# The last norm of a hybrid decoder block: rows on VectorE alone, fetched by GpSimd's queue, the last bias one expert sooner

## The chip, the cores and the metric

The kernel runs on one core of a Trainium2 chip. The time is the device time of one execution in microseconds (us); the median of three executions stands for the kernel. A profile of one execution, taken on the chip, gives the trace that is read here. Engines are named as the profile names them: PE (TensorE), PEld (its weight loads), DVE (VectorE), ACT (ScalarE), POOL (GpSimd), and SP (SyncE, which only issues DMAs here). SPq and POOLq are the DMA queues of these engines.

## The reference, cut to what matters

The block takes 512 tokens of 1024 features through a token mixer and a norm, then through a mixture of 32 experts of which each token uses 4, adds a gate by an input embedding (`ple`), and ends with a layer norm over all 1024 features:

```python
def expert_block(args):
    toks, e = args
    xb = x_pad[toks]
    hgu = xb @ w_gate_up[e] + b_gate_up[e]
    gate = jnp.minimum(hgu[:, :D_FF], SWIGLU_LIMIT)
    up = jnp.clip(hgu[:, D_FF:], -SWIGLU_LIMIT, SWIGLU_LIMIT)
    act = (up + 1.0) * gate * jax.nn.sigmoid(SWIGLU_ALPHA * gate)
    return act @ w_down[e] + b_down[e]
...
    ple = jax.nn.sigmoid(h @ w_ple_gate[i]) * (p[i].astype(h.dtype) @ w_ple_proj[i])
    h = layer_norm(DN_ALPHA * h + y + ple, ln_moe_g[i], ln_moe_b[i])
```

`y` is the sum over a token's four experts, weighted by the router. All is float32.

## The kernel before

The first third of the time is the token mixer. From about 700 us on, a loop runs over 32 places `e`; at each place one expert is done, in an order that a sort of the experts by their number of tokens gives (`RANKS`). A place is long (a first block of 64 tokens and a second of 32) or short (the first block alone); `SHORT_AT` lists the 13 short places, which take the experts with the fewest tokens. A block of 64 tokens fills PE by halves: the two halves of a weight's columns go to the two halves of the output's 128 partitions.

At each place SP loads 12 units of 1024 KB: 8 with the rows of `w_gate_up` (128 input features each) and 4 of `w_down`. The units go round 18 buffers, so SP runs ahead of PE. PE multiplies units 1 to 4 in order. In a short place the last four units are then multiplied twice, first for the left 256 columns and then for the right (`LATE`), so that ACT and DVE can work on the left half (`activate`: one sigmoid on ACT, three instructions on DVE) while PE does the right one. Then PE turns the result (`turned`), multiplies by the 4 units of `w_down` into `po`, ACT scales `po` by the router's weight into `og`, and POOL's queue adds `og` to the rows of `y_d` in DRAM (`indirect_dma_start` with `compute_op=ALU.add`, the scatter).

Each place up to 29 also does one or two of 32 pieces of the embedding gate (`embed`).

The last norm needs the finished rows. The last place, 31, is short and is treated apart: its 64 tokens' rows are fetched from `y_d` into `yr` in the expert's own layout, get the expert's output on the chip, and are normed there (`last_rows`). All 512 rows as they stand without expert 31 are fetched into four tiles `yts[0..3]` (named H in the trace), normed (`norm_steps`, with `row_stats` for the statistics and `normed` for the two passes) and written to `out`; then `yr` overwrites the 64 rows that expert 31 touches, by a scatter that waits for the four writes.

The norm is cut into steps, which the calls of `take_step` between PE's products place in the program: `NORM_AT` empty steps, then the characters of `STEPS`. A digit below 4 is the statistics of tile n (`first`), a digit 4 + n its norm (`second`), a blank an empty step. `AFTER` steps are left for `last_rows`, beneath the wait for its square root on POOL. `keep` holds these instructions in the order of the program on their engine. Tiles in `POOL_ROWS` are normed by one ACT and two POOL instructions, the others by two DVE instructions.

The gain and the bias of the last norm have to stand on all 128 partitions. `spread` does that: SP loads the vector into row 0 of the tile `lasts["bias"]` (bb in the trace), PE multiplies a column of ones by it (`pbr`, line 161), ACT copies the product (line 162). Gain and bias use the same row in turn:

```python
def spread(dst, vec):
    row = lasts["bias"][0:1, :]
    nc.sync.dma_start(row, vec.rearrange("(o d) -> o d", o=1))
    broadcast_row(dst, row)
```

A DMA queue's instructions are issued in order: SP or POOL stands at an instruction until what it waits for is there, and what is written behind it stands too. At place 31 the kernel before first issues the 8 units of `w_gate_up` and three of `w_down` (`FETCH_AT`), then the fetch of the four tiles, then the load of the bias, and the last unit.

Of the kernel before, what the change touches and what calls it, by code (L numbers as in the profile page):

```python
# [16 lines left out]
ALU = mybir.AluOpType  # L17
# [4 lines left out]
P = 128  # L22
# [22 lines left out]
BLOCKS = ((0, 64), (64, 32))  # L45
CAP = 96
SHORT_CAP = 64
SHORT_AT = (2, 4, 7, 9, 12, 14, 16, 19, 21, 24, 26, 29, 31)
SHORT = len(SHORT_AT)
FIXED = 2  # L50

# [8 lines left out]

TABLES_AT = 3


NORM_AT = 25
STEPS = "0 142 5367"
POOL_ROWS = (0, 1)
FETCH_AT = 3
AFTER = 2


# [14 lines left out]
def blocks(e):  # L85

    return [(i, first, n, P // n) for i, (first, n) in enumerate(BLOCKS[:1] if IS_SHORT[e] else BLOCKS)]
# [8 lines left out]
def block_kernel(ctx: ExitStack, tc: tile.TileContext, a: dict, out: bass.AP):  # L96
# [120 lines left out]
    def row_stats(pool, src, m=P, keep=lambda ins: ins, bufs=1):  # L217

        st = pool.tile([m, 2, 6], F32, name="ln_st", tag="ln_st")
        for i in range(2):  # L220
            keep(v_.bn_stats(st[:, i, :], src[:, i * 512:(i + 1) * 512]))
        mv = pool.tile([m, 2], F32, name="ln_mv", tag="ln_mv", bufs=bufs)
        keep(v_.bn_aggr(mv, st))
        rs = pool.tile([m, 1], F32, name="ln_rs", tag="ln_rs", bufs=bufs)
        keep(v_.tensor_scalar(rs, mv[:, 1:2], LN_EPS, None, op0=ALU.add))
        g_.tensor_tensor(rs, rs, mhalf[:m, 0:1], op=ALU.pow)
        return mv[:, 0:1], rs

    def normed(dst, src, stats, gb, bb, keep=lambda ins: ins):
        mean, rs = stats  # L230
        keep(v_.scalar_tensor_tensor(dst, src, mean, gb, op0=ALU.subtract, op1=ALU.mult))  # L231
        keep(v_.scalar_tensor_tensor(dst, dst, rs, bb, op0=ALU.mult, op1=ALU.add))  # L232
# [1078 lines left out]
    def unit(src):  # L1311
        u = units[ctr[0] % len(units)]
        ctr[0] += 1
        if u in (vg_pool, ring, ring3, hT, split):
            raw = u.tile(list(src.shape), F32, name="raw", tag={hT: "A", split: "parts"}.get(u, "raw"))
        else:
            raw = u if len(src.shape) == 2 else u.rearrange("p (j d) -> p j d", j=src.shape[1])
        load = nc.sync.dma_start(raw, src)
        if FREE <= ctr[0] <= len(units):
            tc.keep_in_program_order(load)  # L1320
        return raw
# [8 lines left out]
    def columns_of(t, i):  # L1330

        return t[:, :D // 2] if i == 0 else t[:, D // 2:]
# [19 lines left out]
# [5 lines that stand above are left out]

    def fetch_rows():
        for n in range(NT):
            fetched = nc.sync.dma_start(yts[n], y_d[n * P:(n + 1) * P, :])  # L1360
        return fetched

    keep = tc.keep_in_program_order

# [6 lines left out]
    def norm_steps():  # L1371
        got = {}

        def first(n):
            mean, rs = got[n] = row_stats(ep, yts[n], keep=keep, bufs=NT + 1)
            if n in POOL_ROWS:
                g_.tensor_tensor(mean, mean, rs, op=ALU.mult)
                g_.tensor_scalar(mean, mean, -1.0, None, op0=ALU.mult)

        def second(n):  # L1380
            if n in POOL_ROWS:
                shift, rs = got[n]
                keep(s_.activation(yts[n], yts[n], AF.Identity, scale=rs, bias=shift))
                g_.tensor_tensor(yts[n], yts[n], gb3, op=ALU.mult)
                g_.tensor_tensor(yts[n], yts[n], lasts["bias"], op=ALU.add)
            else:
                normed(yts[n], yts[n], got[n], gb3, lasts["bias"], keep)
            nc.sync.dma_start(out[n * P:(n + 1) * P, :], yts[n])

        def wait():  # L1390
            pass

        side.extend([wait] * NORM_AT)
        for c in STEPS:
            side.append(wait if c == " " else lambda c=c: (first if c < "4" else second)(int(c) % 4))

    def rows_of(e, i):
        return bass.IndirectOffsetOnAxis(ap=sidx[:, e, i:i + 1], axis=0)
# [6 lines left out]
    def half_rows(dst, src):  # L1405

        for j in range(2):
            r = slice(j * SHORT_CAP, (j + 1) * SHORT_CAP)
            s_.activation(dst[r, :], src[r, j * 512:(j + 1) * 512], AF.Copy)
# [44 lines left out]
    def expert(e):  # L1454
# [9 lines left out]
        def rows_up(k):  # L1464
            return wg_e[:, k * P:(k + 1) * P, :].rearrange("o p c -> p (o c)")

        def rows_down(u):
            return wd_e[:, 2 * u * P:(2 * u + 2) * P, :].rearrange("o (p j) d -> p (o j) d", j=2)
# [37 lines left out]
        last = e == NE - 1  # L1506
        down_order = (0, 2, 1, 3) if last else range(4)
        if last:

            raws = [unit(rows_up(k)) for k in range(KD)]  # L1510
            raws_down = [unit(rows_down(u)) for u in down_order[:FETCH_AT]]
            yr = rows_to_add_to(e)
            fetched = fetch_rows()
            norm_steps()
        late = []
        for k in range(KD):
            if e == 0 and k == TABLES_AT:
                first_tables()
                xg = gather(1)
                main_tables(2)  # L1520
            raw = raws[k] if last else unit(rows_up(k))
            late.append((k, raw))
            if k < KD - LATE:
                up(k, raw)
                if k == KD - LATE - 1:
                    for old in late:
                        up_more(*old)
                    late = []
# [17 lines left out]
        if e == NE - 2:  # L1546
# [2 lines left out]
            lasts["gain2"] = plp.tile([P, NT, P], F32, name="stg").rearrange("p n c -> p (n c)")  # L1549
            spread(gb3, a["ln_moe_g"][0])  # L1550
            half_rows(lasts["gain2"], gb3)
        if e == NE - 1:
            spread(lasts["bias"], a["ln_moe_b"][0])

        while len(done) < min(e + 1 + (e >= NE - 7) + (e >= NE - 5), NE):
            embed(len(done))
# [5 lines left out]
        products(first, po, pick.to_broadcast([P, first[2]]), bias_down, True)  # L1562
        todo = []
        for i, u in enumerate(down_order):
            if not last:
                raw = unit(rows_down(u))
            elif i < FETCH_AT:
                raw = raws_down[i]
            else:
                with tc.issue_after(fetched.ins):  # L1570
                    raw = unit(rows_down(u))
            if last and i == 1:
                turned(sgs, as_, first, range(2, 4), True)
            for h in range(2):
                products(first, po, tokens(as_, 2 * u + h, first), raw[:, h:h + 1, :], stop=i == 3 and h == 1)
                take_step()
                todo.append((2 * u + h, raw[:, h:h + 1, :]))
        if xg is not None:
            turn_tokens(xg, e + 1)
        for block in more:  # L1580
# [2 lines left out]
            for k, w in todo:  # L1583
                products(block, pq, tokens(as_, k, block), w, stop=k == KD - 1)
        og = ep.tile([P, D // 2 + D // 4], F32, name="og", tag="og")
        for i, _, n, parts in blocks(e):
            s_.activation(columns_of(og, i), (po, pq)[i][:, :D // parts] if i else po, AF.Copy, scale=wslot[:, e, i:i + 1])  # L1587
        if e == NE - 1:
            bias2 = xs.rearrange("p k t -> p (k t)")[:, :D // 2]
            half_rows(bias2, lasts["bias"])  # L1590
            while len(side) > AFTER:
                take_step()
            last_rows(e, po, yr, lasts["gain2"], bias2)
            return og
        for i, _, n, parts in blocks(e):
            g_.indirect_dma_start(out=by_parts(y_d, parts), out_offset=rows_of(e, i), in_=columns_of(og, i), in_offset=None,  # L1596
# [84 lines left out]
```

## Time and profile before

| | us |
|---|---|
| median of three executions | 1797.73 |
| lowest and highest of them | 1795.44, 1806.05 |
| the profiled execution, as timed | 1802.86 |
| its span in the profile | 1801.1 |
| PE busy | 1725.2 (96%) |
| DVE busy | 557.4 (31%) |
| ACT busy | 409.0 (23%) |
| POOL busy | 196.3 (11%) |

The span runs from the first to the last instruction of the profiled execution; the timed value is 1.8 us more. Times below are positions in this span. The busy shares are averages over stages with different limits: what a change in the last 60 us is worth is read from the instructions there.

### The profile page before, as it was taken

How to read it: one execution, taken by the hardware profiler on the slowest of the kernel's cores; microseconds unless marked ns; L12 is line 12 of the kernel's file. 1: busy time of each engine (PE TensorE's matmuls, PEld its weight loads, DVE VectorE, ACT ScalarE, POOL GpSimd, SP SyncE). 2: the span in 40 equal slices, each digit the busy share in tenths (PEclk: the TensorE clock that was granted, in tenths of full speed). 3: DMA queues.
4: the chain of work that ended last, by engine and by line, in shares of the span. 5: the costliest groups of instructions: out<-in, count | busy, mean ns of one | idle time of the engine just before them, and what ended most of it. 6: DMA issues, size and time to landing. Idle time of an engine off the chain costs nothing. (4 is left out here: it accounts for less than half of the span.)

```text
span 1801.1 us, 26079 instructions
## 1 busy us (share of the span) xinstructions
PE 1725.2 (96%) x10591; PEld 973.9 (54%) x10591; DVE 557.4 (31%) x1326; ACT 409.0 (23%) x653; POOL 196.3 (11%) x202
## 2 busy tenths in 40 slices
PE   6999999999998999999999999999999999999994
PEld 5888887888886873344343434334343434334422
DVE  7566455436334654111121111111111102102104
ACT  3665455334322321011011011011010101101111
POOL 1000000000000101102011102102010101110113
PEclk9999999999998989999999999999999999999997
DMA  8322232322218477999999999999999998999993
GB/s 267 107 70 71 71 136 99 140 94 71 94 71 297 167 282 300 359 414 356 408 361 406 406 370 355 409 413 380 410 409 388 405 411 316 415 362 412 408 370 133
DMA packets 127642, 513.93 MB, mean 285 GB/s; under 512 B 14434, under 2 KB 44546, under 8 KB 78228
## 3 DMA queue, kind: packets, MB, share of 16 engines
q1 hardware_dynamic: 95988, 466.11, 64.6%
q0 software_dynamic: 16160, 29.63, 6.8%
q10 hardware_dynamic: 15360, 16.39, 2.7%
q8 instruction: 86, 1.41, 0.3%
q14 instruction: 48, 0.39, 0.1%
HBM read 484.36 MB, written 27.72 MB: 284 GB/s over the span
## 5 line engine op out<-in xcount | busy, mean ns | idle before, releaser
L1452 PE MATMUL pg<-raw,turned 128*64 128x512 f32 (+1 forms) x2120 | 423.2, 532 | 4.1 <-DVE up L1502 3.7
L1452 PEld LDWEIGHTS pg<-raw,turned 128*64 128x64 f32 x2120 | 149.4, 137 | 240.6 <-issue 200.9
L1502 DVE TENSOR_SCALAR up<-pg 128x256 f32<-128x256 f32 (+1 forms) x45 | 24.2, 537 | 708.2 <-PE pg L1452 708.2
L1452 PE MATMUL pq<-raw,turned 128*32 128x512 f32 (+1 forms) x2000 | 198.3, 498 | 0.0
L1452 PE MATMUL po<-raw,turned 128*64 128x512 f32 x784 | 175.9, 597 | 0.0
L182 PE MATMUL proj<-parts_w,H 128*128 128x512 f32 x640 | 161.7, 398 | 0.0
L182 PE MATMUL proj<-H,parts_w 128*128 128x512 f32 x640 | 157.4, 394 | 3.3 <-ACT vt L499 1.9
L174 DVE TENSOR_TENSOR parts_w<-raw,parts_w 128x1024 fp32r<-128x1024 f32 x84 | 102.5, 1222 | 154.5 <-ACT parts_w L172 154.0
L1500 ACT ACTIVATE sgs<-pg 128x256 f32<-128x256 f32 (+1 forms) x45 | 21.3, 474 | 543.7 <-PE pg L1452 543.7
L1596 POOL DMA_INDIRECT y_d<-og,sidx x50 | 80.0, 1600 | 526.6 <-ACT og L1587 321.7
L182 PEld LDWEIGHTS proj<-parts_w,H 128*128 128x128 f32 x640 | 121.2, 191 | 25.1 <-DVE H L939 0.3
L182 PEld LDWEIGHTS proj<-H,parts_w 128*128 128x128 f32 x640 | 119.1, 188 | 28.2 <-ACT vt L499 2.3
L172 ACT ACTIVATE parts_w<-raw 128x1024 fp32r<-128x1024 f32 x84 | 88.7, 1059 | 178.0 <-PE proj L184 172.1
L1452 PEld LDWEIGHTS pq<-raw,turned 128*32 128x32 f32 x2000 | 55.3, 109 | 124.3 <-issue 106.6
L1452 PEld LDWEIGHTS po<-raw,turned 128*64 128x64 f32 x784 | 55.1, 138 | 97.7 <-issue 93.3
L184 PE MATMUL proj<-parts_w,H 128*128 128x512 f32 x320 | 84.0, 393 | 0.0
L1326 POOL DMA_INDIRECT xg<-h_d,gidx x49 | 50.4, 1029 | 295.6 <-PE ptr L1342 248.5
L184 PE MATMUL proj<-H,parts_w 128*128 128x512 f32 x320 | 80.5, 390 | 0.0
L1587 ACT ACTIVATE og<-po,wslot 128x512 f32<-128x512 f32 x32 | 22.0, 687 | 214.1 <-PE po L1452 199.9
L184 PEld LDWEIGHTS proj<-parts_w,H 128*128 128x128 f32 x320 | 60.8, 190 | 12.9
L184 PEld LDWEIGHTS proj<-H,parts_w 128*128 128x128 f32 x320 | 59.9, 188 | 12.4
L1037 PE MATMUL ple<-rawg,H 128*128 128x128 f32 x512 | 62.4, 275 | 0.0
(351 smaller groups left out, 1800.0 us busy)
## 6 DMA issues: line engine op xcount, KB each, us to landing
raw<-in_w_gate_up_dram SPq DMA_DIRECT2D x223, 1024.0 KB
raw<-in_w_down_dram SPq DMA_DIRECT2D x98, 1024.0 KB
raw<-in_w_in_dram SPq DMA_DIRECT2D x36, 1024.0 KB
hr<-in_w_gate_up_dram SPq DMA_DIRECT2D x22, 1024.0 KB
hr<-in_w_down_dram SPq DMA_DIRECT2D x20, 1024.0 KB
gb<-in_w_gate_up_dram SPq DMA_DIRECT2D x11, 1024.0 KB
gb<-in_w_down_dram SPq DMA_DIRECT2D x10, 1024.0 KB
raw<-in_w_proj_a_dram SPq DMA_DIRECT2D x4, 1024.0 KB
```

The source lines that it names most:

```text
L172: s_.activation(hi, src, AF.Copy)
L174: v_.tensor_tensor(lo, src, f32(hi), op=ALU.subtract)
L182: t_.matmul(ps, wh if keep else x, x if keep else wh, start=st, stop=False)
L184: t_.matmul(ps, wl if keep else xh, xh if keep else wl, start=False, stop=stop)
L1037: t_.matmul(pg[:, :P], H2[:, k, t], emb["gate"][:, k, :], start=(k == 0), stop=(k == KD - 1))
L1326: g_.indirect_dma_start(out=columns_of(xg, i), out_offset=None, in_=by_parts(h2_d, parts), in_offset=bass.IndirectOffsetOnAxis(ap=gidx[:, ...
L1452: t_.matmul(dst, x, cols, start=start, stop=stop, skip_group_check=closed)
L1500: s_.activation(dst, gate, AF.Sigmoid, scale=SW_ALPHA)
L1502: v_.tensor_scalar(tmp, up, LIMIT + 1.0, 1.0 - LIMIT, op0=ALU.min, op1=ALU.max)
L1587: s_.activation(columns_of(og, i), (po, pq)[i][:, :D // parts] if i else po, AF.Copy, scale=wslot[:, e, i:i + 1])
L1596: g_.indirect_dma_start(out=by_parts(y_d, parts), out_offset=rows_of(e, i), in_=columns_of(og, i), in_offset=None, compute_op=ALU.add)
```

## The change

Five edits are made together.

1. `SHORT_AT`: the short places 16, 21, 26 and 29 become 17, 22, 27 and 30. The last two places are now both short; place 29 is long.
2. The fetch of the four tiles goes from SP's queue to POOL's, in front of the fetch of `yr`. Nothing on SP waits for it, so the units of place 31 are loaded one by one in their order (`FETCH_AT`, `raws` and `issue_after` go).
3. All four tiles are normed on DVE (`POOL_ROWS` goes). `STEPS` has no blanks; the calls of `take_step` at place 31 take all of it but the last digit ahead of `last_rows`.
4. `spread` of the bias stands at the end of place 30's second products; `half_rows`, which copies it into the layout of `yr`, stays at place 31.
5. ACT's scaling of the last `po` into `og`, which only the rare overflow path needs, comes behind `last_rows`.

```diff
-SHORT_AT = (2, 4, 7, 9, 12, 14, 16, 19, 21, 24, 26, 29, 31)
+SHORT_AT = (2, 4, 7, 9, 12, 14, 17, 19, 22, 24, 27, 30, 31)
...
-STEPS = "0 142 5367"
-POOL_ROWS = (0, 1)
-FETCH_AT = 3
+STEPS = "01234567"
 AFTER = 2
...
     def fetch_rows():
         for n in range(NT):
-            fetched = nc.sync.dma_start(yts[n], y_d[n * P:(n + 1) * P, :])
-        return fetched
+            g_.dma_start(yts[n], y_d[n * P:(n + 1) * P, :])
...
         def first(n):
-            mean, rs = got[n] = row_stats(ep, yts[n], keep=keep, bufs=NT + 1)
-            if n in POOL_ROWS:
-                g_.tensor_tensor(mean, mean, rs, op=ALU.mult)
-                g_.tensor_scalar(mean, mean, -1.0, None, op0=ALU.mult)
+            got[n] = row_stats(ep, yts[n], keep=keep, bufs=NT + 1)
 
         def second(n):
-            if n in POOL_ROWS:
-                shift, rs = got[n]
-                keep(s_.activation(yts[n], yts[n], AF.Identity, scale=rs, bias=shift))
-                g_.tensor_tensor(yts[n], yts[n], gb3, op=ALU.mult)
-                g_.tensor_tensor(yts[n], yts[n], lasts["bias"], op=ALU.add)
-            else:
-                normed(yts[n], yts[n], got[n], gb3, lasts["bias"], keep)
+            normed(yts[n], yts[n], got[n], gb3, lasts["bias"], keep)
             nc.sync.dma_start(out[n * P:(n + 1) * P, :], yts[n])
...
         if last:
-
-            raws = [unit(rows_up(k)) for k in range(KD)]
-            raws_down = [unit(rows_down(u)) for u in down_order[:FETCH_AT]]
+            fetch_rows()
             yr = rows_to_add_to(e)
-            fetched = fetch_rows()
             norm_steps()
...
-            raw = raws[k] if last else unit(rows_up(k))
+            raw = unit(rows_up(k))
...
-        if e == NE - 1:
-            spread(lasts["bias"], a["ln_moe_b"][0])
+        if last:
+            bias2 = xs.rearrange("p k t -> p (k t)")[:, :D // 2]
+            half_rows(bias2, lasts["bias"])
...
+        if e == NE - 2:
+            spread(lasts["bias"], a["ln_moe_b"][0])
         if xg is not None:
             turn_tokens(xg, e + 1)
...
-        for i, _, n, parts in blocks(e):
-            s_.activation(columns_of(og, i), (po, pq)[i][:, :D // parts] if i else po, AF.Copy, scale=wslot[:, e, i:i + 1])
-        if e == NE - 1:
-            bias2 = xs.rearrange("p k t -> p (k t)")[:, :D // 2]
-            half_rows(bias2, lasts["bias"])
+        if last:
             while len(side) > AFTER:
                 take_step()
             last_rows(e, po, yr, lasts["gain2"], bias2)
+        for i, _, n, parts in blocks(e):
+            s_.activation(columns_of(og, i), (po, pq)[i][:, :D // parts] if i else po, AF.Copy, scale=wslot[:, e, i:i + 1])
+        if last:
             return og
```

SP's queue, before, from the third `w_down` unit of place 31 to the writes of the result (H is the four fetched tiles, bb the row that takes gain and bias, raw a unit of weights):

```order
L1318 DMA raw<-in_w_down_dram 128x2048
L1360 DMA H_9433<-y_d 128x1024 x4
L1355 DMA bb_16495<-in_ln_moe_b_dram 1x1024
L1318 ISA
L1318 DMA raw<-in_w_down_dram 128x2048
L1618 TENSOR_LOAD over
L1618 ISA x2
L1388 DMA out_dram<-H_9433 128x1024 x4
```

The same queue now, from the last `w_down` unit of place 30 to the first unit of place 31:

```order
L1315 DMA raw<-in_w_down_dram 128x2048
L1352 DMA bb_16534<-in_ln_moe_b_dram 1x1024
L1444 TENSOR_LOAD order
L1444 ISA x2
L1315 ISA
L1315 DMA raw<-in_w_gate_up_dram 128x2048
```

The load of the bias row stood behind 11 of the 12 units of place 31 and now stands ahead of all 12; the fetch of H has left this queue for POOL's, where it stands between the scatter of place 30 and the fetch of `yr`.

DVE, before, from the last statistics of the fetched tiles on; a second pair like the last two rows follows, and then the two passes over `yr`:

```order
L225 TENSOR_SCALAR ln_rs<-ln_mv 128x1
L1412 SCALAR_TENSOR_TENSOR yr<-po,wslot,yr 128x512
L1415 BN_STATS last_st<-yr 128x6
L1416 BN_AGGR last_mv<-last_st 128x2
L1421 TENSOR_TENSOR last_mv<-last_mv,pboth 128x1
L1422 TENSOR_TENSOR last_mv<-last_mv 128x1
L1423 SCALAR_TENSOR_TENSOR last_mr<-last_mv,pboth 128x1
L1424 COPY last_mr<-pboth 128x1
L231 SCALAR_TENSOR_TENSOR H_9433<-H_9433,ln_mv,pT 128x1024
L232 SCALAR_TENSOR_TENSOR H_9433<-H_9433,ln_rs,bb_16495 128x1024
```

DVE now, from the third of the three pairs that stand behind the statistics:

```order
L228 SCALAR_TENSOR_TENSOR H_9433<-H_9433,ln_mv,pT 128x1024
L229 SCALAR_TENSOR_TENSOR H_9433<-H_9433,ln_rs,bb_16534 128x1024
L1399 SCALAR_TENSOR_TENSOR yr<-po,wslot,yr 128x512
L1402 BN_STATS last_st<-yr 128x6
L1403 BN_AGGR last_mv<-last_st 128x2
L1408 TENSOR_TENSOR last_mv<-last_mv,pboth 128x1
L1409 TENSOR_TENSOR last_mv<-last_mv 128x1
L1410 SCALAR_TENSOR_TENSOR last_mr<-last_mv,pboth 128x1
L1411 COPY last_mr<-pboth 128x1
L228 SCALAR_TENSOR_TENSOR H_9433<-H_9433,ln_mv,pT 128x1024
L229 SCALAR_TENSOR_TENSOR H_9433<-H_9433,ln_rs,bb_16534 128x1024
```

Three pairs of passes over whole tiles now stand ahead of the step that takes `po`, where none stood, and one pair instead of two stands behind it.

## Rows read from the trace of the kernel before

**Rows 1.** Waits of PE's weight loads, 640 to 1752 us: total, times, longest.

```profile
PEld pg L1452 <- DMA raw<-in_w_gate_up_dram: 2.2, 4, 0.8
```

**Rows 2.** Chain that ended last: start, us, what.

```profile
1782.33 3.23 DVE H L231
```

**Rows 3.** Timeline of DVE, place 31 and the end: start, us, what [idle before <-releaser].

```profile
1766.39 0.42 DVE L1502 TENSOR_SCALAR up<-pg 128x256 f32<-128x256 f32 x1 [2.90 <-PE pg L1452]
...
1767.44 0.42 DVE L1504 SCALAR_TENSOR_TENSOR sgs<-pg,sgs 128x256 f32<-128x256 f32 x1
...
1774.21 0.15 DVE L225 TENSOR_SCALAR ln_rs<-ln_mv 128x1 f32<-128x1 f32 x1
1779.09 0.75 DVE L1412 SCALAR_TENSOR_TENSOR yr<-po,wslot,yr 128x512 f32<-128x512 f32 x1 [4.72 <-ACT og L1587]
...
1786.85 1.28 DVE L231 SCALAR_TENSOR_TENSOR H<-H,ln_mv,pT 128x1024 f32<-128x1024 f32 x1
1788.23 1.29 DVE L232 SCALAR_TENSOR_TENSOR H<-H,ln_rs,bb 128x1024 f32<-128x1024 f32 x1
```

**Rows 4.** Timeline of POOL, places 28 to 31 and the end.

```profile
1680.29 1.59 POOL L1596 DMA_INDIRECT y_d<-og,sidx  x1 [0.30 <-issue]
...
1690.41 1.60 POOL L1596 DMA_INDIRECT y_d<-og,sidx  x1 [7.24 <-DMA y_d<-og,sidx]
...
1759.80 1.01 POOL L1402 DMA_INDIRECT yr<-y_d,sidx  x1 [2.98 <-DMA y_d<-og,sidx]
...
1779.71 2.35 POOL L1384 TENSOR_TENSOR H<-H,pT 128x1024 f32<-128x1024 f32 x1
...
1784.43 1.53 POOL L1425 TENSOR_TENSOR last_mr<-last_mr,mhalf 128x1 f32<-128x1 f32 x1
1793.44 1.11 POOL L1429 DMA_INDIRECT out_dram<-yr,sidx  x1 [7.48 <-DMA out_dram<-H]
```

**Rows 5.** Timeline of SP's queue, places 30 and 31: issue start, us over all issues.

```profile
1700.73 0.30 SPq L1355 DMA_DIRECT2D bb<-in_ln_moe_g_dram  x1
1701.23 3.78 SPq L1318 DMA_DIRECT2D raw<-in_w_down_dram  x4
...
1726.35 7.08 SPq L1318 DMA_DIRECT2D raw<-in_w_down_dram  x3
1759.26 1.76 SPq L1360 DMA_DIRECT2D H<-y_d  x4
1761.12 0.29 SPq L1355 DMA_DIRECT2D bb<-in_ln_moe_b_dram  x1
```

**Rows 6.** Timeline of PE, places 29 to 31.

```profile
1694.62 3.86 PE L1452 MATMUL pg<-raw,turned 128*64 128x256 f32 x32 [0.53 <-DVE up L1502]
1698.40 0.51 PE L1342 MATMUL ptr<-ident,sgs 128*128 128x128 f32 x2
...
1734.93 1.98 PE L161 MATMUL pbr<-bb,ones_f 1*128 1x512 f32 x4
...
1751.43 5.37 PE L1452 MATMUL pg<-raw,turned 128*64 128x512 f32 x24
...
1768.58 1.95 PE L161 MATMUL pbr<-bb,ones_f 1*128 1x512 f32 x4 [1.79 <-DMA bb<-in_ln_moe_b_dram]
```

**Rows 7.** Timeline of ACT: the scaling of `po` at places 27, 28, 29.

```profile
1638.64 0.69 ACT L1587 ACTIVATE og<-po,wslot 128x512 f32<-128x512 f32 x1 [6.88 <-PE po L1452]
...
1678.25 0.69 ACT L1587 ACTIVATE og<-po,wslot 128x512 f32<-128x512 f32 x1 [6.82 <-PE po L1452]
...
1708.68 0.69 ACT L1587 ACTIVATE og<-po,wslot 128x512 f32<-128x512 f32 x1 [6.88 <-PE po L1452]
```

**Rows 8.** Windows: busy us (instructions) of PE, PEld, DVE, ACT, POOL; granted clock, DMA share, GB/s.

```profile
680.00:683.00 3.00, 0.00 (x0) 0.00 (x0) 2.93 (x7) 0.00 (x0) 0.00 (x0) 0.99 1.02 431
683.00:686.00 3.00, 2.79 (x9) 0.77 (x8) 3.00 (x10) 0.00 (x0) 0.00 (x0) 0.50 1.02 431
...
1640.00:1706.00 66.00, 65.47 (x502) 28.62 (x496) 10.38 (x35) 6.23 (x15) 10.37 (x8) 1.00 1.02 409
```

More of the change, by code (lines that the diff above doesn't have):

```diff
@@ L1394, in norm_steps @@
         for c in STEPS:
-            side.append(wait if c == " " else lambda c=c: (first if c < "4" else second)(int(c) % 4))
+            side.append(lambda c=c: (first if c < "4" else second)(int(c) % 4))
     def rows_of(e, i):
@@ L1564, in expert @@
         for i, u in enumerate(down_order):
[L1565 to L1571, printed above, removed]
+            raw = unit(rows_down(u))
             if last and i == 1:
```

## The prediction, made before the changed kernel ran

> **What bounds the kernel now.** I read the waits first, to see whether PE starves in the expert phase. In 1112 us its weight loads wait for `w_gate_up` units 2.2 us in all [rows 1], and PE is busy 65.5 of 66 us in a stretch near the end while the DMA engines move 409 GB/s [rows 8]. So PE sets the pace of the places, and the weights arrive ahead of it. The work of the places is the same after the change: as many long and short ones, in another order. Only the end can change much.
>
> I read the chain next: it enters at 1782.33 us on DVE, in a pass over one of the fetched tiles [rows 2]. The timelines of the engines give what lies around it. DVE ends the activation of place 31 at 1767.86; I call this moment A. It ends the four statistics at 1774.36 and stands 4.72 us until ACT has scaled the last `po` [rows 3]. From the step on `po` to the scalars of its norm it takes 3.24 us (1779.09 to 1782.33) [rows 2, 3]. Its first pass over a tile then takes 3.23 us against 1.28 later [rows 2, 3], while POOL runs its own passes of 2.35 us [rows 4]. POOL's queue holds the square root until 1784.43 and takes 1.53 us for it [rows 4]. DVE ends the last tile at 1789.52 [rows 3]; the write of that tile holds the scatter of `yr` until 1793.44 [rows 4], and 7.66 us later the span ends. From A to the end: 33.24 us.
>
> **The norm on DVE alone.** From A on, DVE has four statistics (6.50 us), three pairs of passes at 2.67 us (1786.85 to 1789.52, without POOL beside it) [rows 3], the step on `po` with its scalars (3.24), one more pair (2.67), then the write and the scatter's start (3.92) and the rest (7.66): 6.50 + 8.01 + 3.24 + 2.67 + 3.92 + 7.66 = 32.00 us. For the same A that is 1.2 us less than now. The square root fits beneath the fourth pair even at 1.53 us [rows 4]. ACT's scaling that goes behind `last_rows` and the two removed ACT passes cost nothing and gain nothing, because DVE is late by then. DVE reaches `po` at A + 14.5 us. Now PE is done about 11 us after A (the step started at 1779.09), and it loses a wait of 1.79 us and a broadcast of 1.95 us between the products [rows 6]. So PE has some 7 us in hand, and the end depends on A: each us of A is a us of the result.
>
> **The broadcast one expert sooner, and the order of the last places.** PE does the bias (1.95 to 1.98 us [rows 6]) between places 30 and 31. ACT's two copies then stand ahead of the turning of place 31's tokens, for which I allow 1 us. Against it stands the order of the last three places: `po` of place 28 is scaled at 1678.25; a long place after a long one takes 39.61 us and a short one after a long one 30.43 us [rows 7]. In the 30.43 us lies a piece of the embedding gate, which place 30 does not have; the broadcast of the gain comes in its place, and I set them equal. So place 30 ends its `po` at 1717.86 + 30.43 = 1748.3, and place 31 starts at about 1751.3, where it starts now (1751.43 [rows 6]). If nothing else were late, A would stay at 1767.9. The other moved short places (17, 22, 27) I cost at nothing: a swap with the neighbour leaves the sum of PE's work, and the lead of the weights covers one swap [rows 1].
>
> **SP's queue: the wait that comes in.** Now SP issues 11 of the 12 units of place 31 by 1733.4, and only then stands until 1759.26 for the fetch; the bias load comes after it [rows 5]. After the change the bias load stands ahead of all 12 units. It writes the row that holds the gain, so it waits until PE has read the gain in place 30, and 12 MB of weights wait behind it. When is that? In the short place 29 of the trace, PE turns the activation 20.15 us after ACT scaled `po` of the place before (1678.25 to 1698.40 [rows 6, 7]). In place 30 the gain's broadcast stands there: 1717.86 + 20.15 = 1738.0, with the turning (0.5) and the broadcast (1.98) 1740.5. By then the four `w_down` units of place 30 have long landed: the gain's own load waits for the last embedding piece, 9 us later than now (1700.73 [rows 5]) because place 29 is long, and four units take 10 us. So the DMA engines stand idle for some 15 us.
>
> From 1740.5 on, allow 0.5 us for reading the expert's number and 2 us until the first unit flows (a scatter on nearly idle engines takes 2.98 us [rows 4]). A unit of 1024 KB at 409 GB/s takes 2.56 us [rows 8]. Unit 8 lands at 1743 + 8 x 2.56 = 1763.5 if nothing else is on the engines. When is it needed? After it come a quarter of the left half (0.97 us by the right half's 3.86), the wait and the right half (0.53 + 3.86) [rows 6], and the activation (1766.39 to 1767.86) [rows 3]: A = landing + 6.8. The weights hide as long as unit 8 lands by 1761.0. They don't: 2.5 us are missing without other traffic.
>
> And there is other traffic now. The scatter of place 30 starts at about 1749.5; on loaded engines it lands 8.5 us after its issue (1681.88 to 1690.41 [rows 4]), so at about 1759.5 POOL can issue the four fetches, 1 us each by the row of `yr` [rows 4]. They bring 2.1 MB, 5.1 us of the engines' time at 409 GB/s, just where units 7 to 12 are on the way. If the weights went first, unit 8 would land at 1763.5; if all the fetched rows and the scatter (1 us) went first, at 1769.6. At 1760 some 6.6 units are there; 1.4 more at half the rate take 7 us, so 1767. I take 1766.5, between the two, nearer to sharing because the loaded scatter took 8.5 us against 2.98 [rows 4].
>
> [...]
>
> **The sum.** A = 1766.5 + 6.8 = 1773.3, the end 1773.3 + 32.0 = 1805.3: 4.2 us more than the span of 1801.1. The profiled execution took 1802.9, which is 5.1 above the median of the three runs; 4.2 on the median of 1797.7 gives **1802 us**. Hidden behind DVE: units 9 to 12 land until about 1779.5 and PE ends at about 1781.5, while DVE comes to `po` at 1787.8.
>
> **The rivals.** First, *no stall*. If SP's wait ends some 3 us sooner, or the fetched rows take nothing from the weights, A stays at 1767.9 and the new norm keeps its 1.2 us: 1796.5. For it speaks that unit 8 misses by 2.5 us only, within the error of my place 29; against it, the 2.1 MB on the same engines.
>
> [...]
>
> Third, *late rows*. If the fetch itself takes 17 us on the loaded engines, the fourth tile comes after DVE wants it at A + 4.9 = 1778.2, and every us beyond is a us of the result. At 1 us each of issue and 5.1 to 10 us of shared transfer the rows are there by 1774. A delay of 3 us gives 1805.
>
> Fourth, *the change does not do what it says*: the fetch leaves SP, but SP is not free for it, since the bias row takes the fetch's place as the thing that SP stands for. That is in the forecast already. Were the lead of the weights also broken in the middle (places 17, 22, 27), each break would cost a few us of PE's wait; the 2.2 us of all such waits now [rows 1] say that it has room.
>
> **How the numbers follow.** Forecast 0.47, no stall 0.24, clock 0.18, late rows 0.07, a break in the middle 0.04. The range runs from 1794 (no stall, less the 2.3 us by which the lowest run lies under the median) to 1810 (clock and full sharing). A difference of 1% is about what a measurement of this kernel can tell from none. 1% is 18 us, above 1815.7 or under 1779.8: the clock case would need the late rows and the weights still later to get there, and nothing in these sums comes near the other side. Faster 0.01, same 0.93, slower 0.06.
>
> **What would show it.** SP's timeline: the bias load at about 1740, right after PE's broadcast of the gain, and all units of place 31 behind it. Windows: DMA nearly idle from about 1724 to 1742, then full until about 1780. PE waits for `w_gate_up` units 5 to 8 in place 31, some 5 us in all. DVE: no pause from A to the end except for `po`'s scalars, passes over tiles at 1.28 us each, A at about 1773. I am wrong if the bias load is issued at 1730 or sooner, if PE has no such wait, or if DVE waits for PE's last products; and wholly wrong if places before 29 take another time than now.

## The result, and the profile after

The changed kernel takes 1809.67 us (median of 5 runs, 1805.99 to 1811.21) against 1797.88 us for the kernel before, which ran beside it (5 runs, 1795.44 to 1806.05). The medians lie 11.8 us apart; the ratio of all the runs is 1.0051, with a 95% interval of 1.0028 to 1.0073: some 9 us slower, well inside 1%. The profiled execution took 1809.67 us with a span of 1807.9, against 1802.9 and 1801.1 before.

Executions of one kernel differ by several us, and before place 28 only the order of a few places has changed: in the ten traces of this document ACT scales `po` of place 28 between 1673.7 and 1680.6. So inside the traces I compare **the stretch**: from that moment to the end of the span. It starts at 1678.25 before [rows 7] and at 1677.97 after, so it is 122.85 us before and 129.93 after: 7.1 us longer, of which A (the end of place 31's activation on DVE) is 8.2 us later and the tail from A to the end 1.1 us shorter.

SP's queue after, by its timeline (start, us over all issues):

```profile
1709.36 0.31 SPq L1352 DMA_DIRECT2D bb<-in_ln_moe_g_dram  x1
1709.87 2.32 SPq L1315 DMA_DIRECT2D raw<-in_w_down_dram  x4
1739.13 0.26 SPq L1352 DMA_DIRECT2D bb<-in_ln_moe_b_dram  x1
1740.44 1.40 SPq L1315 DMA_DIRECT2D raw<-in_w_gate_up_dram  x3
...
1745.28 9.35 SPq L1315 DMA_DIRECT2D raw<-in_w_down_dram  x4
```

What it stood for, by the waits of SP's queue, 1680 to 1805 us (total, times, longest):

```profile
SPq L1352 <- PE pbr L158: 26.8, 1, 26.8
```

Before, 11 of the 12 units of place 31 were issued ahead of the long stand [rows 5]. Now the load of the bias row stands 26.8 us for PE's broadcast of the gain, and all 12 units stand behind it. The DMA engines run dry, as the windows of 2 us (one of 8) show: busy us (instructions) of PE, PEld, DVE, ACT, POOL; granted clock, DMA share, GB/s.

```profile
1724.00:1726.00 2.00, 2.00 (x12) 0.72 (x10) 0.00 (x0) 0.00 (x0) 0.75 (x1) 1.00 0.03 8
...
1738.00:1740.00 2.00, 2.00 (x9) 0.80 (x9) 0.27 (x1) 1.69 (x4) 0.00 (x0) 1.00 0.01 2
...
1742.00:1744.00 2.00, 2.00 (x14) 0.57 (x10) 0.00 (x0) 0.00 (x0) 0.00 (x0) 1.00 0.96 385
...
1764.00:1766.00 2.00, 0.29 (x4) 0.00 (x0) 0.00 (x0) 0.00 (x0) 0.00 (x0) 0.72 1.00 416
1766.00:1768.00 2.00, 1.03 (x6) 0.66 (x8) 0.00 (x0) 0.00 (x0) 0.00 (x0) 0.50 1.04 430
1768.00:1770.00 2.00, 1.47 (x10) 0.46 (x8) 0.91 (x2) 0.38 (x1) 0.00 (x0) 0.50 1.02 420
...
1772.00:1780.00 8.00, 7.86 (x48) 3.74 (x47) 5.40 (x13) 2.41 (x5) 1.13 (x2) 1.00 0.91 371
```

PE's timeline shows where this is paid:

```profile
1737.12 1.98 PE L158 MATMUL pbr<-bb,ones_f 1*128 1x512 f32 x4
...
1739.70 7.03 PE L1439 MATMUL po<-raw,turned 128*64 128x512 f32 x32
...
1749.92 5.37 PE L1439 MATMUL pg<-raw,turned 128*64 128x512 f32 x24 [0.69 <-ACT turned L1340]
...
1757.74 1.08 PE L1439 MATMUL pg<-hr,turned 128*64 128x256 f32 x8 [0.73 <-DMA hr<-in_w_gate_up_dram]
1760.24 1.08 PE L1439 MATMUL pg<-hr,turned 128*64 128x256 f32 x8 [1.42 <-DMA hr<-in_w_gate_up_dram]
1763.21 1.08 PE L1439 MATMUL pg<-raw,turned 128*64 128x256 f32 x8 [1.88 <-DMA raw<-in_w_gate_up_dram]
1766.97 1.98 PE L1439 MATMUL pg<-raw,turned 128*64 128x256 f32 x8 [2.68 <-DMA raw<-in_w_gate_up_dram]
1769.47 1.97 PE L1439 MATMUL pg<-hr,turned 128*64 128x256 f32 x8 [0.53 <-DVE up L1489]
```

Units 5 to 8 are late by 0.73 + 1.42 + 1.88 + 2.68 = 6.71 us. Then the granted clock is 0.50, and the eight products of unit 8 take 1.98 us where those of unit 7 took 1.08. Place 31 itself starts at 1749.92, before at 1751.43 [rows 6].

That earlier start is no gain of the change. Before, PE's clock had fallen in place 30, by its timeline

```profile
1734.26 0.74 PE L1342 MATMUL ptr<-ident,sgs 128*128 128x128 f32 x4 [1.04 <-DVE sgs L1504]
...
1737.52 5.29 PE L1452 MATMUL po<-raw,turned 128*64 128x512 f32 x16
```

and by a window:

```profile
1738.00:1740.00 2.00, 2.00 (x8) 0.55 (x6) 0.00 (x0) 0.72 (x2) 0.00 (x0) 0.50 1.03 430
```

Sixteen products for `po` took 5.29 us there, where the 32 of place 30 now take 7.03, with the granted clock at 1.00. So some 1.7 us of the 122.85 are the lower clock of that one execution.

DVE after, by its timeline, from the end of place 31's activation:

```profile
1775.37 0.42 DVE L1491 SCALAR_TENSOR_TENSOR sgs<-pg,sgs 128x256 f32<-128x256 f32 x1
...
1782.21 1.28 DVE L228 SCALAR_TENSOR_TENSOR H<-H,ln_mv,pT 128x1024 f32<-128x1024 f32 x1
...
1789.95 0.74 DVE L1399 SCALAR_TENSOR_TENSOR yr<-po,wslot,yr 128x512 f32<-128x512 f32 x1
...
1792.90 1.28 DVE L228 SCALAR_TENSOR_TENSOR H<-H,ln_mv,pT 128x1024 f32<-128x1024 f32 x1
1794.28 1.28 DVE L229 SCALAR_TENSOR_TENSOR H<-H,ln_rs,bb 128x1024 f32<-128x1024 f32 x1
```

A is 1775.37 + 0.42 = 1775.79. Behind it DVE works on end to end, but for 0.74 us ahead of `po`'s scalars: the step on `po` waits for nothing now, where it waited 4.72 us [rows 3], and the pass that took 3.23 us [rows 2] takes 1.28. From A to the end it is 32.11 us, before 33.24.

POOL's timeline:

```profile
1747.75 1.55 POOL L1576 DMA_INDIRECT y_d<-og,sidx  x1 [15.16 <-ACT og L1572]
1757.49 2.22 POOL L1357 DMA_DIRECT2D H<-y_d  x4 [8.19 <-DMA y_d<-og,sidx]
...
1799.60 1.08 POOL L1416 DMA_INDIRECT out_dram<-yr,sidx  x1 [5.02 <-SPq L1602]
```

The scatter of place 30 lands in 8.2 us beside the weights, and the four fetches are issued right behind it, at 0.55 us each.

ACT's scaling of `po` at places 28, 29 and 30, by its timeline:

```profile
1677.97 0.69 ACT L1572 ACTIVATE og<-po,wslot 128x512 f32<-128x512 f32 x1 [6.88 <-PE po L1439]
...
1717.31 0.69 ACT L1572 ACTIVATE og<-po,wslot 128x512 f32<-128x512 f32 x1 [6.82 <-PE po L1439]
...
1746.79 0.69 ACT L1572 ACTIVATE og<-po,wslot 128x512 f32<-128x512 f32 x1 [5.85 <-PE po L1439]
```

The long place now takes 39.34 us and the short one 29.48.

### The profile page after: what moved, and what is told of

It reads as the page before. It is cut to its first block, busy times and chain, and to the rows that moved or that the text cites. A ratio compares the mean times of both kernels' runs of the same rounds, so it can differ in the third digit from the quotient of the medians.

```text
span 1807.9 us, 26061 instructions
## 1 busy us (share of the span) xinstructions
PE 1726.3 (95%) x10591; PEld 975.8 (54%) x10591; DVE 560.5 (31%) x1330; ACT 407.0 (23%) x651; POOL 190.2 (11%) x198
## 5 line engine op out<-in xcount | busy, mean ns | idle before, releaser
L181 PEld LDWEIGHTS proj<-H,parts_w 128*128 128x128 f32 x320 | 59.9, 188 | 12.3
## 6 DMA issues: line engine op xcount, KB each, us to landing
raw<-in_w_gate_up_dram SPq DMA_DIRECT2D x223, 1024.0 KB, 19.8
raw<-in_w_down_dram SPq DMA_DIRECT2D x98, 1024.0 KB, 19.8
gb<-in_w_gate_up_dram SPq DMA_DIRECT2D x11, 1024.0 KB, 20.4
```

The source lines that it names most:

```text
L181: t_.matmul(ps, wl if keep else xh, xh if keep else wl, start=False, stop=stop)
```

## The experiments

My theory: the whole loss comes from the bias row's load on SP's queue ahead of place 31's weights, and nothing else in the change costs more than 1 or 2 us. The rivals: the order of the last places, the norm on DVE, or the fetched rows that share the engines with the weights carry a part of it. All times below are of the stretch (before 122.85, after 129.93) unless said otherwise, each from one trace; the ratio is that of the timed runs to the kernel before.

| kernel | A from the stretch's start | tail from A | stretch | ratio [95%] |
|---|---|---|---|---|
| before | 89.61 | 33.24 | 122.85 | 1 |
| after | 97.82 | 32.11 | 129.93 | 1.0051 [1.0028, 1.0073] |
| after, bias row loaded by ACT | 88.53 | 31.90 | 120.43 | 0.9989 [0.9976, 1.0001] |
| after, bias back at place 31 | 87.34 | 32.28 | 119.62 | 0.9987 [0.9972, 1.0002] |
| before, bias early | 91.73 | 35.91 | 127.64 | 1.0022 [1.0008, 1.0036] |
| after, fetch behind unit 8 | 97.46 | 31.27 | 128.73 | 1.0037 [1.0022, 1.0051] |
| after, old places | 94.30 | 33.71 | 128.01 | 1.0031 [1.0017, 1.0045] |
| after, norm split as before | 98.30 | 31.53 | 129.83 | 1.0035 [1.0020, 1.0050] |
| before, new places | 85.73 | 36.43 | 122.16 | 0.9996 [0.9982, 1.0010] |
| bias at 31, one tile on ACT and POOL | 87.42 | 31.90 | 119.32 | 0.9972 [0.9957, 0.9988] |

**The bias row loaded by ACT's queue.** All else as after.

```diff
-    def spread(dst, vec):
+    def spread(dst, vec, queue=nc.sync):
-        nc.sync.dma_start(row, vec.rearrange("(o d) -> o d", o=1))
+        queue.dma_start(row, vec.rearrange("(o d) -> o d", o=1))
-            spread(lasts["bias"], a["ln_moe_b"][0])
+            spread(lasts["bias"], a["ln_moe_b"][0], nc.scalar)
```

> The changed kernel with one edit: the row of the bias is loaded by ACT's queue instead of SP's, so that SP does not stand for PE's reading of the gain. Measured from ACT's scaling of place 28's po to the end of the span, the kernel before takes 122.9 us and the changed kernel 129.9. Theory (SP's wait for the gain's row starves place 31): units of place 31 are issued from about 1711 on, no wait for weights in place 31, clock stays at 1.00, A (end of the last activation) falls from 1775.8 to about 1768, the stretch to 122 us, the time by 8 us. Rival one (the norm on DVE alone costs the time): DVE's chain from A is the same 32 us, but A would not move, so the stretch stays at 129 to 130. Rival two (the fetched rows take the engines from the weights): A falls by 3 us at most, 127.

SP's timeline in this kernel:

```profile
1713.96 6.13 SPq L1315 DMA_DIRECT2D raw<-in_w_gate_up_dram  x3
...
1721.48 1.20 SPq L1315 DMA_DIRECT2D hr<-in_w_gate_up_dram  x2
1742.41 0.91 SPq L1315 DMA_DIRECT2D raw<-in_w_gate_up_dram  x2
```

and ACT's:

```profile
1740.93 0.49 ACTq L1352 DMA_DIRECT2D bb<-in_ln_moe_b_dram  x1
```

Six units of place 31 now go out between 1713.96 and 1722.7. SP still stands ahead of units 7 and 8, by its waits from 1680 to 1799 us:

```profile
SPq L1315 <- DMA bb<-in_ln_moe_b_dram: 19.5, 1, 19.5
```

Why these two wait for the bias row the record does not show; with six units ahead they come in time all the same. ACT reaches the load behind its own copies of the gain's broadcast, and the issue takes 0.49 us. PE has no wait for `w_gate_up` in place 31 any more, and the stretch is 9.5 us shorter than after, 1.6 below what I expected. Place 31 starts 72.10 us into the stretch here (1750.87) and 71.95 after, so A is 9.3 us sooner through the weights alone: 6.7 us of waits, and of the rest 2.0 us by my estimate are products, which in the trace after took that much longer at the granted clock of 0.50 (the last quarter of the left half 1.98 us instead of 0.97, the right half 4.8 instead of 3.86).

**The load and the broadcast of the bias back at place 31.**

```diff
+        if last:
+            spread(lasts["bias"], a["ln_moe_b"][0])
             bias2 = xs.rearrange("p k t -> p (k t)")[:, :D // 2]
...
-        if e == NE - 2:
-            spread(lasts["bias"], a["ln_moe_b"][0])
```

> The changed kernel with the edit on the bias undone: load and broadcast of the bias stand at place 31 again, behind the 8 units of w_gate_up on SP. Theory: no starved units as in the run with the bias on ACT's queue, and the broadcast's 2 us on PE no longer lie ahead of place 31, so A is some 2 us sooner still: about 1766, the stretch 120 us, 3 us less than the kernel before and 10 less than the changed one. PE's end moves 2 us later than with the bias on ACT's queue but stays ahead of DVE. Rival one (norm on DVE alone): 129 to 130. Rival two (contention of the fetched rows): 127.

119.62: as expected, 10.3 us less than after. The loss belongs to this one part. What is left of the change then beats the kernel before by 3.2 us of the stretch; the timed ratio of 0.9987 has 1 just inside its interval. (In this trace too place 30 ran longer: from the start of the gain's broadcast to the end of the 24th product for `po` it is 9.5 us, in the kernel before with the new places, further down, 7.9. I put these 1.6 us down to a lower clock, by the 5.29 us of the products above.)

**The kernel before with only the bias early.**

```diff
-        if e == NE - 1:
-            spread(lasts["bias"], a["ln_moe_b"][0])
...
+        if e == NE - 2:
+            spread(lasts["bias"], a["ln_moe_b"][0])
```

> The kernel before with one edit: load and broadcast of the bias at the end of place 30. Place 30 is long here, so the gain is read at about 1737 and all 12 units of place 31 wait for that; but the fetch stands behind 11 of them on SP. Theory: unit 8 lands at about 1760.5, just when it is needed (the broadcast itself moves place 31 by 2 us), so no or one us of starving; the fetched rows come late, at 1769 to 1773, and DVE's statistics with them; the stretch is 123 to 125 us (before 122.9). Rival (the early bias costs the 7 us by itself, whatever stands beside it): 129 to 130.

127.64, 4.8 us over before: a miss, between my figure and the rival's. SP's timeline:

```profile
1765.25 1.76 SPq L1360 DMA_DIRECT2D H<-y_d  x4
1767.21 0.34 SPq L1318 DMA_DIRECT2D raw<-in_w_down_dram  x1
```

and the waits of PE, 640 to 1805 us:

```profile
PE po L1452 <- DMA raw<-in_w_down_dram: 4.0, 1, 4.0
...
PE pg L1452 <- DMA raw<-in_w_gate_up_dram: 1.1, 1, 1.1
```

I had counted only the lateness of unit 8, which is 1.1 us. Here the fetch still stands on SP, behind the eleven late units: it goes out 89.5 us into the stretch, before 81.0 (1759.26 [rows 5]), and the last `w_down` unit behind it, for which PE waits 4.0 us. So the tail grows by 2.7 us too. In this order of places the bias costs half of what it costs in the changed kernel. In both traces sixteen products for `po` in place 30 take the longer time (5.30 us here, 5.29 before, where the window shows 0.50), which delays place 31 and so hides some of the wait for weights; by my estimate, with the 1.7 us from above, the cost without it would be 6.5.

**The fetch on SP again, behind unit 8.**

```diff
-            g_.dma_start(yts[n], y_d[n * P:(n + 1) * P, :])
+            nc.sync.dma_start(yts[n], y_d[n * P:(n + 1) * P, :])
...
-            fetch_rows()
             yr = rows_to_add_to(e)
...
+        if last:
+            fetch_rows()
         for i, u in enumerate(down_order):
```

> The changed kernel with the fetch of the four tiles on SP's queue behind unit 8 of place 31, so that the rows take nothing from units 1 to 8. Theory: they took about 3 us and, by the stall, pushed the clock down; unit 8 lands at about 1764 instead of 1767, the stalls before it shrink from 6.7 to 3 to 4 us, the clock may stay at 1.00, A comes at about 1771, the stretch is 125 to 126 us. The rows land by 1770 and DVE does not wait for them. Rival (only SP's wait counts, sharing costs nothing): 129 to 130, with unit 8 at 1767 as now.

128.73: a miss. PE's timeline at units 7 and 8:

```profile
1762.50 1.08 PE L1439 MATMUL pg<-raw,turned 128*64 128x256 f32 x8 [1.39 <-DMA raw<-in_w_gate_up_dram]
1765.69 1.97 PE L1439 MATMUL pg<-raw,turned 128*64 128x256 f32 x8 [2.11 <-DMA raw<-in_w_gate_up_dram]
```

and a window:

```profile
1766.00:1768.00 2.00, 1.67 (x8) 0.47 (x4) 0.29 (x1) 0.38 (x1) 0.00 (x0) 0.50 1.02 408
```

Unit 8 comes 88.02 us into the stretch, after 89.00: the fetch took 1.0 us from the weights, not the 3 us that I had put on it. (The kernel with the split norm, below, moves the same bytes up to there as the changed one and has unit 8 at 89.23, so two such traces agree to 0.2 us.) The waits are still 5.7 us (0.81 + 1.42 + 1.39 + 2.11), and the clock still falls.

**The old order of places in the changed kernel.**

```diff
-SHORT_AT = (2, 4, 7, 9, 12, 14, 17, 19, 22, 24, 27, 30, 31)
+SHORT_AT = (2, 4, 7, 9, 12, 14, 16, 19, 21, 24, 26, 29, 31)
```

> The changed kernel with the old list of short places (29 short, 30 long). From ACT's scaling of place 28's po to the end it takes 129.9 us now, the kernel before 122.9, the kernel before with the early bias 127.6. Theory: SP still stands for the gain's row, so place 31 still starves, but the gain is read about 2 us sooner against place 28 and place 31 starts later; A falls by about 6 us against the changed kernel, and the scatter of the long place 30 ends later, so the fetched rows come up to 5 us after A: 124 to 128 us. Rival (the new order of the places makes the loss by itself): back to 122 to 123.

128.01, at the upper edge of the 124 to 128 expected. The bias load goes out 58.32 us into the stretch (1736.61) instead of 61.16, while place 31 starts at the same time (72.03 and 71.95), so the weights have 2.8 us more and A is 3.5 us sooner. Of that, 1.6 us is lost behind A: place 30 is long and has two scatters, POOL issues the fetch at 1765.47 only, and DVE waits 0.77 + 0.91 us for the first rows. Here the lower clock came behind two short waits, by PE's timeline

```profile
1760.36 1.08 PE L1439 MATMUL pg<-raw,turned 128*64 128x256 f32 x8 [1.22 <-DMA raw<-in_w_gate_up_dram]
1763.11 1.98 PE L1439 MATMUL pg<-raw,turned 128*64 128x256 f32 x8 [1.67 <-DMA raw<-in_w_gate_up_dram]
```

and by the windows:

```profile
1764.00:1766.00 2.00, 1.47 (x8) 0.53 (x6) 0.76 (x2) 0.38 (x1) 0.53 (x1) 0.50 1.03 413
```

**The norm of two tiles on ACT and POOL again, in the changed kernel.**

```diff
-STEPS = "01234567"
+STEPS = "0 142 5367"
+POOL_ROWS = (0, 1)
...
+            if n in POOL_ROWS:
+                shift, rs = got[n]
+                keep(s_.activation(yts[n], yts[n], AF.Identity, scale=rs, bias=shift))
+                g_.tensor_tensor(yts[n], yts[n], gb3, op=ALU.mult)
+                g_.tensor_tensor(yts[n], yts[n], lasts["bias"], op=ALU.add)
+            else:
+                normed(yts[n], yts[n], got[n], gb3, lasts["bias"], keep)
```

> The changed kernel with the norm of two tiles on ACT and POOL again and the old steps. Theory: A stays at 97.8 us after place 28's po, because the norm does not touch the weights; from A on DVE has less to do and comes to po right when PE ends, 7 us after A, so the tail is about 30 us instead of 32: 127 to 128.5 us (now 129.9). Rival (the norm on DVE alone is what costs): 122 to 123.

129.83, the same as after: the norm is not the loss. The 127 to 128.5 of the expectation is missed, since the split saves DVE less than 1 us. DVE's timeline has two long passes

```profile
1784.05 3.45 DVE L229 SCALAR_TENSOR_TENSOR H<-H,ln_mv,pT 128x1024 f32<-128x1024 f32 x1
...
1788.79 3.36 DVE L229 SCALAR_TENSOR_TENSOR H<-H,ln_mv,pT 128x1024 f32<-128x1024 f32 x1
```

beside POOL's:

```profile
1784.08 2.34 POOL L1381 TENSOR_TENSOR H<-H,pT 128x1024 f32<-128x1024 f32 x1
...
1787.88 3.19 POOL L1382 TENSOR_TENSOR H<-H,bb 128x1024 f32<-128x1024 f32 x1
```

DVE saves four passes of 1.28 us and loses 2.17 + 2.08 us in the two it keeps. The tail is 31.53 us, 0.6 less than after; but the four kernels above whose DVE does the whole norm and waits for no rows (the changed one among them) have tails from 31.27 to 32.28, so the two norms cannot be told apart here. With A this late the split would have done no worse.

**The new order of places in the kernel before.** The edit is the line `SHORT_AT` above, the other way round.

> The kernel before with the new list of short places alone (30 short, 29 long). Theory: the order costs nothing by itself; place 31 starts about 1 us sooner after place 28's po, the units of place 31 are issued behind no wait but the buffers', no wait for w_gate_up in place 31: 121 to 124 us (before 122.9). Rival (two short places at the end need 24 MB in less time than the engines take, whatever SP does): PE waits for units 5 to 8 some 3 us or more, 126 us or more.

122.16, as expected, and PE has no wait for `w_gate_up` in place 31: the rival is out. A is 3.9 us sooner, 1.7 of them because the products in place 30 were not slowed (20 for `po` in 4.46 us, where 16 took 5.29). The waits of DVE, 1755 to 1797 us, show where it goes:

```profile
DVE yr L1412 <- ACT og L1587: 8.3, 1, 8.3
```

As before, PE has the bias row, its broadcast and all products for `po` ahead of it, and in the old norm DVE holds its own passes back until `po` is there. But this wait was 4.72 us before [rows 3], and most of what it has grown by is products that ran longer, by PE's timeline

```profile
1760.86 3.30 PE L161 MATMUL pbr<-bb,ones_f 1*128 1x512 f32 x4 [2.06 <-DMA bb<-in_ln_moe_b_dram]
...
1764.51 3.62 PE L1452 MATMUL po<-raw,turned 128*64 128x512 f32 x8
```

where before the broadcast took 1.95 us [rows 6] and the same eight products

```profile
1770.70 1.88 PE L1452 MATMUL po<-raw,turned 128*64 128x512 f32 x8
```

That is 3.1 us, which I put down to a lower clock, since at 0.50 the products of unit 8 took 1.98 us instead of 1.08 in the trace after. With 1.7 us of lower clock in the one trace and 3.1 in the other, the difference of 0.7 does not tell what the order of the places is worth by itself; it only rules out a large loss.

**The bias at place 31, and one tile of four on ACT and POOL.** The edit is that of the second experiment with that of the sixth, with two other lines:

```diff
-STEPS = "01234567"
+STEPS = "01 42 3567"
+POOL_ROWS = (0,)
```

> The kernel with the bias back at place 31 (119.6 us) and, besides, one of the four tiles normed by ACT and POOL, one tile on DVE ahead of po and two behind it. Theory: A as there (87.3 us after place 28's po), and DVE's chain from A loses a pair of passes (2.67 us) less what POOL's passes cost DVE: 117 to 119 us, the time 4 us or so under the kernel before. If POOL's two passes slow DVE by as much as they save: 119.6 as there.

119.32 and a ratio of 0.9972 [0.9957, 0.9988], the only one whose interval lies below 1. The second branch of the expectation holds, by DVE's timeline

```profile
1775.89 3.09 DVE L230 SCALAR_TENSOR_TENSOR H<-H,ln_rs,bb 128x1024 f32<-128x1024 f32 x1 [0.20 <-DVE H L229]
```

and POOL's:

```profile
1774.54 3.37 POOL L1381 TENSOR_TENSOR H<-H,pT 128x1024 f32<-128x1024 f32 x1 [2.63 <-ACT H L1380]
```

What POOL takes over it takes back from DVE's next pass (3.09 us instead of 1.28). In the stretch it leads the kernel with all four tiles on DVE by 0.3 us only, and the intervals of the two ratios overlap; whether its lead is real these runs do not tell.

## Why the prediction was right

The forecast was 4.2 us more in the trace; the spans differ by 6.8, the stretches by 7.1, the timed ratio says 9 with an interval of 5 to 13. No measurable change by the bound of 1% was right, the sign too, and the mechanism is the one forecast; its size was short by some 3 us. The median of 1809.67 lies 0.3 us inside the range, and two of the five runs lie above it: that it came in is partly luck. What separates it from 1802 beyond those 3 us is within the scatter of the executions of one kernel (1795 to 1806 before).

The parts add up along one path of the runs: new places in the kernel before, 122.85 to 122.16, -0.7; norm on DVE and fetch on POOL, to 119.62, -2.5; the bias one expert sooner, to 129.93, +10.3. The sum is +7.1. The traces at the ends of these steps each hold some lower clock on the path that counts: 1.7 us before, 3.1 with the new places alone, 1.6 with the bias back at place 31, 2.0 after (0.50 in the windows of before and after, read from the times of the products in the other two). So the first two parts are no larger than what the clock alone does between two traces, and the timed ratios of the two kernels (0.9996 and 0.9987) have 1 in their intervals: neither part is shown. The third stands far outside; less the clock on both sides it is an estimated 9.9. On another path the parts differ: in the old order of places the bias alone costs 4.8. The parts are not independent, because the wait costs what the lead of place 31's weights does not cover, and the order of places bears on that lead.

By the steps of the prediction:

- **SP's wait.** The bias load was put at 1740.5 and stood until 1739.13; the idle DMA engines, the units behind it and the waits for units 5 to 8 (some 5 us forecast, 6.7 measured) came as written. Both runs that took the load away from the head of place 31's units gave back all of it.
- **Unit 8.** Put at 1766.5, used at 1766.97, but by two errors that nearly cancel. Unit 5 comes at 1757.74, 0.25 us after the first fetch is issued (1757.49) and no later than in the run with the fetch behind unit 8 (79.77 and 79.86 us into the stretch), where 1743 + 5 x 2.56 gives 1755.8: the first units come 2 us later than forecast. Three more units at 2.5 us (the gap from unit 5 to 6) would give 1765.2, so the fetched rows and whatever else ran beside them cost 1.7 us; the run with the fetch behind unit 8 gave back 1.0 of it. The forecast had 3. Half the rate for the last 1.4 units put unit 8 at 1767, which is where it came; but half of that agreement is the late start. The half was my estimate: how the queues share the engines no run here shows.
- **A = landing + 6.8.** This is the term that was mis-sized. It was measured at 1775.8 - 1767.0 = 8.8: the last quarter of the left half took 1.98 us instead of 0.97, and the right half to its last product 4.8 (1769.47 to 1774.29) instead of 3.86, because the granted clock was 0.50 from 1766 to 1770. The sum had left a lower clock at nothing; it cost 2.0 us, and the clock was at 1.00 again from 1772 on. I had given it a chance of 0.18, with a pause of 3 us [rows 8] as the only fall that I had read; here it came behind four waits, the longest of 2.68, and the trace of before held another fall, behind a wait of 1.04 (the lines above). The 1810 at the top of the range holds a price of the clock that no run shows; the trace after shows these 2.0 us in its place.
- **The tail.** 32.0 forecast, 32.11 measured, with every DVE pass at 1.28 us. Two sizes cancel in it: DVE from A to the end of its last tile took 19.8 us (20.4 forecast, since a pair of passes took 2.57 and the step on `po` with its scalars 2.95), the write and the scatter behind it 12.3 (11.6 forecast). As a gain of the norm on DVE alone the 1.2 us were counted against the wrong thing, though: the 33.24 us of before hold a wait of 4.72 us for `po`, which a late A removes in either form. The split norm on the changed kernel's A gives 31.53. What the new norm is worth where A is early stays open: from the kernel before with the new places, with the norm on DVE alone, its steps in one row, and the fetch on POOL, the stretch is 2.5 us shorter (122.16 to 119.62), but the longer of the two holds 3.1 us of lower clock ahead of `po`, the shorter 1.6 ahead of place 31.
- **The order of places** was set at nothing for the start of place 31: 1751.3 forecast, 1749.92 measured. The short place took 29.48 us, not 30.43. That the forecast met the 1751.43 of before so closely was chance, because that figure holds the 1.7 us of lower clock in place 30.
- **No stall** did not happen. **Late rows** cost nothing in the changed kernel, since the fetch was issued at 1757.49 and DVE never waited for it; with the old places it went out nearly 8 us later and DVE waited 1.7 us for it. **No break in the middle**: PE's waits for weights in its timeline are those of place 31 alone.

What stays open: why the first units land 2 us later than 2.56 us each from 1743; the bytes moved by 1760 would fill 6.9 units (0.8 MB by 1744, then 400 GB/s for 16 us), yet PE gets only the sixth then. Some of these bytes are not weights: the scatter of place 30 was on the engines from 1747.75 to 1757.49, and the first fetched rows behind it; how much they make up no view here tells. Several units are under way at once: the first eight are issued by 1744.62, and from issue to landing they take 12.1 to 16.0 us by the medians of their tiles. Whether the sixth is late by that, no run shows.

## What to carry to other kernels

Before a small load is moved forward in a queue that issues in order, look at what it waits for, and count every byte that is queued behind it: here a row of 1024 numbers stood 26.8 us and took 12 weight transfers with it. A load that reuses a buffer belongs on the queue of the engine that comes late to it anyway (ACT, which had just copied the old contents: 120.43 us instead of 129.93), or at the place where its wait has already passed (119.62). And a wait of PE can have a second price in the products behind it, here 2.0 us at a granted clock of 0.50 behind 6.7 us of waits, so a stall forecast in several pieces should carry some of the lower clock in its sum. Last, read the granted clock along the path in both traces before a difference of 1 to 3 us is put down to an edit.

## What the hardware showed that I had not expected

**The clock fell without one long pause.** With the old places PE waited 1.22 and 1.67 us, with products of 1.08 us between, and the granted clock was 0.50 right behind; in the changed kernel it fell behind waits of 0.73, 1.42, 1.88 and 2.68 us. Before, a single wait of 1.79 us ahead of the bias's broadcast left that at 1.95 us [rows 6] and the granted clock at 1.00, but with the new places in the kernel before a wait of 2.06 us was followed by a broadcast of 3.30 us and products that also ran longer. And before, the wait of 1.04 us in place 30 was followed by the fall shown above, while behind the same wait at the same place of the changed kernel with the old places the 32 products for `po` took 7.03 us, as after at 1.00. Likewise the stretch of place 30 from the gain's broadcast to the 24th product for `po` took 9.5 us with the bias back at place 31 and 7.9 in the kernel before with the new places, though PE does the same work there in both. So the length of one gap does not tell it, and a trace can hold such a fall at a place that the edit does not touch.

**Passes of DVE and POOL that overlapped took nearly both times.** With two tiles on POOL a DVE pass of 1.28 us took 3.45 beside POOL's 2.34, and ended 1.1 us after POOL's; in the last experiment POOL's pass of 2.35 took 3.37, beginning 0.13 us after a DVE pass of 1.28, and the next DVE pass, of 3.09 us, then ended 1.07 us after it. The longer time is nearly the loser's and the winner's added: 1.28 + 2.34 = 3.62 for the 3.45, 2.35 + 1.28 = 3.63 for the 3.37. What holds them up these rows do not show.

**A plain fetch costs POOL little to issue.** Four of 512 KB took 2.22 us on POOL's queue, 0.55 each, where the indirect one of `yr` took 1.03.
